# A two-layer hybrid encoder step: pairs of half products written as a software pipeline, with one fixed order each on PE, ACT and DVE

## The chip, the cores and the metric

One core of a Trainium2 chip runs the whole program. The metric is the device time of one execution in microseconds; the median of three timed runs counts, and a separate execution was profiled.

## What is computed

One inference step of an encoder of two layers (D_MODEL = 1024) for 512 prompt rows and 8 x 16 sample rows, 640 rows in all (T), which share the weights. Cut to what matters here, a layer is

```python
(a_u, a_v, a_g, b_x, b_g, c_q, c_kv, c_kr, c_g, m_q, gate_logits) = split_cols(x @ w_in)
oa, v_rows = gmlp_branch(a_u, a_v, ...);  oa = oa * silu(a_g)
ob, conv_new, h_new = rglru_branch(b_x, ...);  ob = ob * silu(b_g)
oc, ckv_new, kr_new = mla_branch(c_q, c_kv, c_kr, ...);  oc = oc * silu(c_g)
om = mem_attend(m_q, mem_k, mem_v)
g = sigmoid(gate_logits).reshape(B, T, 4, D_MODEL)
merged = g[:,:,0] * (oa @ w_br[:512]) + g[:,:,1] * (ob @ w_br[512:1024]) \
       + g[:,:,2] * (oc @ w_br[1024:1536]) + g[:,:,3] * (om @ w_br[1536:])
x_new = layer_norm(ALPHA * x + merged @ w_out)
```

Every product is done in float32r with the operands split into a high and a low part (high x high, high x low, low x high).

## The kernel before, in words

All activations lie transposed, features on the partitions and the 640 rows in the free dimension, as two halves of TH = 320 columns. The program is written for the Tile framework: it puts each engine's instructions into an order by its own scheduler, hands out buffers from pools and sets the semaphores; `order_only` adds an order between two instructions, with no data behind it.

**A pair.** `fm_pair` (line 363) makes two chunks of 128 output columns of `x @ w_in` (tensor w_fm) at once, by a Strassen-like scheme of seven half products in place of eight. Each product is 12 matmuls of 128x128 by 320 columns (4 blocks of the contraction; high x high, high x low, low x high), in the order p1 to p7. The products read sums of the halves of x (`xt`), which are made ahead, and these weights: p1 and p2 the first weight tile r0 split into wh (ACT, line 146) and wl (DVE, line 147), written w0 below; p3 and p4 the sum tile ws (w1); p5 and p6 the changed r1 (w2); p7 the 512 columns of the changed second half of r0 (w3). "w3's low part" is the DVE instruction of line 147 that makes the low part of w3, over 512 columns. PSUM holds the results: p1, p2, p3, p5 and p7 in one tile fp, p4 and p6 in fp_c. Between the products ACT copies p1 and u (third product) into tile tu and p4 into z1; DVE (line 389) joins them into z0 and z1. The function `take` then gets each finished part for the activation function.

**40 pairs.** Each layer has six early pairs (`gelu_pair`, `silu_pair`), between the projections and the attention, and 14 merge pairs (`merge_pairs`, line 1055). A merge pair makes the gate logits of chunks f and f+1 of one branch (bi; 4 and 6 in branch 0, 0 to 6 in the other three), ACT applies tanh, and then `merge_y` multiplies the branch's output (bhl, high and low part, made by `bsplit` at the branch's first pair; oscr holds it in DRAM) by the weights of these two chunks (w_br, 512 KB for both; in the last branch w_brm, 256 KB): 48 matmuls or 24, in PSUM tiles y. DVE joins gate and y (lines 1034 and 1038) into macc. "y's tile" is the raw tile of w_br or w_brm, "y's cast" and "y's low part" its split, and "y" the product.

**Weights and their buffers.** Every weight tile comes by a DMA on SP's queue into a tile of the tag raw, and is then split:

```python
def wtile(tag, n, name, bufs=2):
    return wp.tile([128, n], F32 if tag in ("raw", "ws") else F32R, tag=tag, name=name, bufs=bufs)

def wraw(src, n=1024):
    raw = wtile("raw", n, "raw", 3)
    nc.sync.dma_start(out=raw, in_=src)
```

So raw has three buffers, wh three, wl two and ws one, and a load waits until the last reader of the buffer that it gets is done. SP issues its DMAs in order.

**Who sets the order.** On PE the products of all pairs are chained by `order_only`, through `tail["p"]`, in the order of the program. Everything else (ACT, DVE, SP, the matmuls of y) is put in order by the scheduler alone, by what is ready first in its own estimate.

Of the kernel before, what the change touches and what calls it, by code (L numbers as in the profile page):

```python
# [9 lines left out]
F32 = mybir.dt.float32  # L10
F32R = mybir.dt.float32r
AF = mybir.ActivationFunctionType
ALU = mybir.AluOpType
# [6 lines left out]
T = NP_ + NS  # L20
# [19 lines left out]
def encoder_step(  # L40
# [5 lines left out]
    nc = tc.nc  # L46
# [33 lines left out]
    def acc(name="acc"):  # L80
        return pa.tile([128, 2, 512], F32, tag="acc", name=name)

    def bank_s(name="ps_s"):
        return pb.tile([128, 512], F32, tag="s", name=name, bufs=2)
# [85 lines left out]
    def order_only(ins_, dep):  # L170
        if dep is not None:
            tc.add_manual_dep(
                ins_.ins, dep.ins.name,
                mybir.DependencyInfo(mybir.DependencyClass.NoSync, mybir.DependencyReason.SCHED_ONLY),
                reason="products of a pair stand in this order on the engine",
            )
# [23 lines left out]
    for l in range(L):  # L200
# [159 lines left out]
            xt[11], xt[21] = ((xh[i][:, :, lo_], xl[i][:, :, lo_]) for i in range(2))  # L360
            xt[22] = xh[1][:, :, hi_], xl[1][:, :, hi_]

        def fm_pair(c, take):

            r0, r1 = (wraw(ins["w_fm"][l, c + e]) for e in range(2))
            ws = wtile("ws", 1024, "ws", 1)
            a_, b_ = slice(0, 512), slice(512, 1024)

            def wsum(out, x, y):
                DVE.tensor_tensor(out=out, in0=x, in1=y, op=ALU.add)  # L370

            ab, bc = acc("fp"), bank_s("fp_c")[:, 0:TH]
            ba, bb = (ab[:, j, 0:TH] for j in range(2))

            def product(o, hl, half, x, first, last):
                bh, bl = xt[x]
                h, lo = hl
                steps = [(k, h, b) for k in range(4) for b in (bh, bl)] + [(k, lo, bh) for k in range(4)]
                for n, (k, a, b) in enumerate(steps):
                    k0 = half * 512 + k * 128  # L380
                    mm = PE.matmul(  # L381
                        out=o, lhsT=a[:, k0:k0 + 128], rhs=b[:, k, :],
                        start=(first and n == 0), stop=(n == len(steps) - 1), skip_group_check=True,
                    )
                    order_only(mm, tail.get("p"))
                    tail["p"] = mm

            def psum(out, x, y, op):
                DVE.tensor_tensor(out=out, in0=x, in1=y, op=op)  # L389

            z0, z1, t_ = ftmp([128, T], "z0"), ftmp([128, T], "z1"), tmp([128, T], "tu")
            p1, u = t_[:, lo_], t_[:, hi_]
            w1 = whl(r0)
            product(ba, w1, 0, 11, True, False)
            ACT.copy(out=p1, in_=ba)  # L395
            product(bb, w1, 1, 21, True, True)
            psum(z0[:, lo_], p1, bb, ALU.add)
            take(0, lo_, z0[:, lo_])
            wsum(ws[:, b_], r0[:, a_], r1[:, a_])
            wsum(r1[:, a_], r1[:, a_], r1[:, b_])  # L400
            wsum(ws[:, a_], r0[:, a_], r1[:, a_])
            w1 = whl(ws)
            product(ba, w1, 0, 2, False, False)
            ACT.copy(out=u, in_=ba)
            product(bc, w1, 1, 3, True, False)
            ACT.copy(out=z1[:, hi_], in_=bc)
            w1 = whl(r1)
            wsum(r0[:, b_], r0[:, b_], ws[:, a_])
            product(ba, w1, 0, 1, False, False)
            psum(z1[:, hi_], z1[:, hi_], ba, ALU.subtract)  # L410
            product(bc, w1, 1, 4, False, True)
            psum(z1[:, lo_], bc, u, ALU.subtract)
            take(1, slice(0, T), z1)
            w4 = whl(r0[:, b_], 512)
            product(ba, w4, 0, 22, False, True)
            take(0, hi_, ba)
            return z0, z1

        def silu_pair(i, c, fm):
            gs = []  # L420
            z = fm_pair(fm + c, lambda e, cols, v_: gs.append((e, cols, v_)))
            th = [tmp([128, T], f"th{e}") for e in range(2)]
            for e, cols, v_ in gs:
                ACT.activation(out=th[e][:, cols], in_=v_, func=AF.Tanh, scale=0.5)
                DVE.scalar_tensor_tensor(
                    out=th[e][:, cols], in0=th[e][:, cols], scalar=1.0, in1=v_, op0=ALU.add, op1=ALU.mult
                )
            for e in range(2):
                nc.gpsimd.dma_start(out=gscr[i][c + e], in_=th[e])

        def gelu_pair(c):
            gs = []
            z = fm_pair(FM_U + c, lambda e, cols, v_: gs.append((e, cols, v_)))
            for e, cols, v_ in gs:
                ACT.activation(out=ub[:, c + e, cols], in_=v_, func=AF.Gelu_apprx_tanh)


        a0, a1 = acc("c01"), acc("c23")
# [72 lines left out]

        am = atile([128, 5120], F32, "am")
        ub = am[:, 2560:5120].rearrange("p (k t) -> p k t", k=4)
        for c in (0, 2):
            gelu_pair(c)


        nc.sync.dma_start(out=am[:, 0:1024], in_=ins["w_mix"][l])
# [16 lines left out]
            layer_norm(v[:, t, :], v[:, t, :], mvv[:, t, 0:1], rv[:, t:t + 1], vlg, vlb)  # L535
        nc.gpsimd.dma_start(out=outs["sv"][l], in_=v[:, 4, :])

        silu_pair(1, 0, FM_CG)


        nc.sync.dma_start(out=ckvT_s[:, :, 0:128], in_=ins["past_ckvT"][l])
# [21 lines left out]
                out=krT_s[r:r + 32, :, 128:144], in_=o[r:r + 32, 384:512].rearrange("p (b t) -> p b t", b=NB)  # L563
            )

        silu_pair(1, 2, FM_CG)


        for c in range(4):
# [17 lines left out]
            DVE.tensor_tensor(out=ub[:, c, :], in0=ub[:, c, :], in1=th, op=ALU.mult)  # L587
        nc.gpsimd.dma_start(out=gscr[0].rearrange("k p t -> p k t"), in_=ub)

        for c in (0, 2):  # L590
            silu_pair(2, c, FM_BG)

        ep = otile([128, 2560], F32, "ep")
        nc.sync.dma_start(out=ep[:, 1024:2304], in_=ins["rope_q"])
# [421 lines left out]
        def bsplit(bi, get):  # L1016
            nk, scale = (2, 1.0) if bi == 3 else (4, 0.5)
            if bi == 3:
                t_ = otile([128, 2, nk, T], F32R, "bhl")
                bhl = [t_[:, 0], t_[:, 1]]  # L1020
            else:
                bhl = [otile([128, nk, T], F32R, f"bhl{j}") for j in range(2)]
            for k in range(nk):
                split(bhl[0][:, k, :], bhl[1][:, k, :], get(k), scale)
            return bhl

        def merge_y(bi, f, g, wh, wl, bhl):
# [12 lines left out]
        def merge_split(f):  # L1040
            mg.append(otile([128, 2, 2, T], F32R, f"mg{f}"))
            for e in range(2):
                split(mg[-1][:, 0, e, :], mg[-1][:, 1, e, :], macc[:, f + e, :], 0.5)
# [8 lines left out]
                merge_y(0, f, g, wh, wl, bhl)  # L1052
                yield bhl

        def merge_pairs(bi, fs, bhl=None):
            br, n = (0, 2, 1, 3)[bi], 256 if bi == 3 else 512
            wsrc = ins["w_brm"][l] if bi == 3 else ins["w_br"][l, br]

            def back(k):
                src = tmp([128, T], "osrc")  # L1060
                nc.gpsimd.dma_start(out=src, in_=oscr[br][k])
                return src

            for f in fs:
                gs = []
                z = fm_pair(22 + br * 8 + f, lambda e, cols, v_: gs.append((e, cols, v_)))
                for e, cols, v_ in gs:
                    ACT.activation(out=z[e][:, cols], in_=v_, func=AF.Tanh, scale=0.5)
                if bhl is None:
                    bhl = bsplit(bi, back)  # L1070
                raw = wtile("raw", 2 * n, "raw", 3)
                nc.sync.dma_start(
                    out=raw.rearrange("p (e c) -> p e c", e=2), in_=wsrc[f:f + 2].rearrange("e p c -> p e c")
                )
                wh, wl = whl(raw, 2 * n)
                for e in range(2):
                    c = slice(e * n, (e + 1) * n)
                    merge_y(bi, f + e, z[e], wh[:, c], wl[:, c], bhl)
                if bi == 3 and f == 0:
                    merge_split(0)  # L1080
            if bi == 3:
                for f in (2, 4, 6):
                    merge_split(f)

        lru_in(0)
        lru_split(0)
# [24 lines left out]
        lru_rest(3)  # L1111
        nc.gpsimd.dma_start(out=outs["lh"][l], in_=lh)
        x_sums_back()
        merge_pairs(0, (4, 6), bhl)
        for bi in (1, 2, 3):
            merge_pairs(bi, (0, 2, 4, 6))


        wo = {}
# [187 lines left out]
```

## Time and profile before

| | |
|---|---|
| median of 3 runs | 1473.69 us (1472.77 to 1473.84) |
| profiled execution | 1476.25 us, its span 1474.5 us |
| mean granted TensorE clock | 0.996 |
| PE, PEld | 94%, 85% of the span |
| DVE, ACT, POOL | 67%, 44%, 8% |
| weight loads in the queue of SP | 108 of w_fm, 20 of w_br (512 KB), 8 of w_brm |

The time of an execution is the span of the profile and what lies around it (1.75 us here). PE is the matmuls, PEld the weight loads that run beside them; DVE is VectorE, ACT ScalarE, POOL GpSimd, SP the engine that issues the loads. In the timeline an instruction's row ends with the time that its engine sat idle before it and with what ended that wait; "issue" is a wait for nothing that the profile shows. The layers' merge stages with pairs lie at about 375 to 665 and 1110 to 1410 us of the span.

### The profile page before, as it was taken

How to read it: one execution, taken by the hardware profiler on the slowest of the kernel's cores; microseconds unless marked ns; L12 is line 12 of the kernel's file. 1: busy time of each engine (PE TensorE's matmuls, PEld its weight loads, DVE VectorE, ACT ScalarE, POOL GpSimd, SP SyncE). 2: the span in 40 equal slices, each digit the busy share in tenths (PEclk: the TensorE clock that was granted, in tenths of full speed). 3: DMA queues.
4: the chain of work that ended last, by engine and by line, in shares of the span. 5: the costliest groups of instructions: out<-in, count | busy, mean ns of one | idle time of the engine just before them, and what ended most of it. 6: DMA issues, size and time to landing. Idle time of an engine off the chain costs nothing. (4 is left out here: it accounts for less than half of the span.)

```text
span 1474.5 us, 22634 instructions
## 1 busy us (share of the span) xinstructions
PE 1383.2 (94%) x8896; PEld 1256.6 (85%) x8896; DVE 984.0 (67%) x1676; ACT 650.2 (44%) x1159; POOL 124.5 (8%) x254
## 2 busy tenths in 40 slices
PE   8998899999999999999999989999999999999997
PEld 8788888788989999988888888876889999998886
DVE  8677757685566566665885776575855565657756
ACT  6453534464634343444255435444555433434430
POOL 1101200021100000000111012000211000000000
PEclk9999999999999999999999999999999999999999
DMA  7624523153233322236374247132533323222343
GB/s 273 247 86 168 194 82 118 57 193 123 87 118 104 90 82 80 72 101 207 107 230 184 85 161 230 30 118 83 183 125 97 103 90 104 84 78 60 108 140 107
DMA packets 59098, 183.95 MB, mean 125 GB/s; under 512 B 6641, under 2 KB 15761, under 8 KB 55921
## 3 DMA queue, kind: packets, MB, share of 16 engines
q1 hardware_dynamic: 48304, 127.54, 27.3%
q0 software_dynamic: 10688, 54.98, 10.3%
q8 instruction: 70, 1.15, 0.3%
q14 instruction: 36, 0.29, 0.1%
HBM read 148.49 MB, written 32.69 MB: 123 GB/s over the span
## 5 line engine op out<-in xcount | busy, mean ns | idle before, releaser
L146 ACT CAST wh<-raw 128x1024 fp32r<-128x1024 f32 (+3 forms) x215 | 198.7, 924 | 244.4 <-PE fp_c L381 84.0
L147 DVE TENSOR_TENSOR wl<-raw,wh 128x1024 fp32r<-128x1024 f32 (+3 forms) x215 | 229.1, 1065 | 106.5 <-issue 41.6
L381 PE MATMUL fp<-xh,wh 128*128 128x320 f32 x480 | 147.3, 319 | 27.1 <-ACT tu L395 23.5
L121 PE MATMUL y<-bhl,wh 128*128 128x320 f32 x896 | 142.6, 310 | 4.3 <-ACT lb L905 3.3
L381 PE MATMUL fp<-xl,wh 128*128 128x320 f32 x480 | 142.6, 309 | 0.0
L121 PEld LDWEIGHTS y<-bhl,wh 128*128 128x128 f32 x896 | 134.0, 188 | 5.1 <-ACT lb L905 3.8
L381 PE MATMUL fp<-xt,wh 128*128 128x320 f32 x640 | 110.9, 315 | 26.3 <-DVE z L389 26.3
L381 PEld LDWEIGHTS fp<-xt,wh 128*128 128x128 f32 x640 | 95.5, 188 | 36.7 <-DVE z L389 36.7
L381 PEld LDWEIGHTS fp<-xh,wh 128*128 128x128 f32 x480 | 90.0, 188 | 38.9 <-ACT tu L395 34.0
L121 PE MATMUL fm<-xl,wh 128*128 128x320 f32 x448 | 114.4, 327 | 0.0
L121 PE MATMUL fm<-xh,wh 128*128 128x320 f32 x448 | 111.7, 323 | 0.0
L381 PE MATMUL fp_c<-xt,wh 128*128 128x320 f32 x640 | 106.9, 309 | 0.0
L381 PEld LDWEIGHTS fp_c<-xt,wh 128*128 128x128 f32 x640 | 97.1, 188 | 0.0
L146 ACT CAST wh<-ws 128x1024 fp32r<-128x1024 f32 x40 | 42.1, 1053 | 115.9 <-DVE ws L370 97.2
L381 PEld LDWEIGHTS fp<-xl,wh 128*128 128x128 f32 x480 | 90.2, 188 | 0.1
L381 PE MATMUL fp<-xh,wl 128*128 128x320 f32 x480 | 89.9, 309 | 0.0
L121 PE MATMUL fm<-xh,wl 128*128 128x320 f32 x448 | 87.2, 327 | 0.0
L121 PEld LDWEIGHTS fm<-xh,wh 128*128 128x128 f32 x448 | 75.5, 188 | 6.8 <-issue 5.2
L121 PEld LDWEIGHTS fm<-xl,wh 128*128 128x128 f32 x448 | 76.2, 189 | 5.9 <-issue 4.7
L121 PE MATMUL y<-bhl,wl 128*128 128x320 f32 x448 | 76.6, 309 | 0.0
L381 PEld LDWEIGHTS fp<-xh,wl 128*128 128x128 f32 x480 | 75.3, 188 | 0.0
L121 PEld LDWEIGHTS fm<-xh,wl 128*128 128x128 f32 x448 | 68.8, 190 | 6.3 <-issue 5.9
(339 smaller groups left out, 2632.2 us busy)
## 6 DMA issues: line engine op xcount, KB each, us to landing
raw<-in_w_fm SPq DMA_DIRECT2D x108, 512.0 KB, 3.7
xsum<-xt POOLq DMA_DIRECT2D x8, 1280.0 KB, 11.0
xt<-xsum POOLq DMA_DIRECT2D x8, 1280.0 KB, 7.3
raw<-in_w_br SPq DMA_DIRECT2D x20, 512.0 KB, 3.9
mcache<-in_mem_kv SPq DMA_DIRECT2D x8, 1024.0 KB, 7.0
raw<-in_w_out SPq DMA_DIRECT2D x16, 512.0 KB, 4.5
osrc<-oscr POOLq DMA_DIRECT2D x20, 320.0 KB, 3.3
gscr<-th POOLq DMA_DIRECT2D x16, 320.0 KB, 2.5
```

Of the source, the lines that this page charges most:

```text
L121: PE.matmul(out=out[:, j, 0:TH], lhsT=a(k), rhs=b(k)[:, j * TH:(j + 1) * TH], start=(n == 0), stop=(n == len(steps) - 1),)
L146: ACT.copy(out=dst_h, in_=src)
L147: DVE.tensor_tensor(out=dst_l, in0=src, in1=dst_h.bitcast(F32), op=ALU.subtract)
L381: mm = PE.matmul(out=o, lhsT=a[:, k0:k0 + 128], rhs=b[:, k, :], start=(first and n == 0), stop=(n == len(steps) - 1), skip_group_check=True,)
```

## The change

`fm_pair` is taken apart. A class `Pair` holds a pair's steps: `load` (r0 and r1), `cast0` and `low0` (w0), `sums`, `cast1` and `low1` (w1). `run_pair(p, nxt, act, y)` writes out the products of pair p and, between them, the steps of the next pair nxt up to its cast1. A class `Branch` holds the steps of y: `cast` (the load of its tile and ACT's cast), `low` and `run`. `on(eng, ins)` chains not only PE's instructions but also ACT's and DVE's of the pairs (copies, casts, low parts, sums, differences, activations), each engine in the order of the program. The instructions of y's product, of bhl, of DVE's joins into macc and of the rest of the layer stay with the scheduler. The early pairs are chained the same way, each writing the next one's steps; `silu_pair` and `gelu_pair` hand their activation functions in as `act`. No instruction's shape changes. The core of the diff:

```diff
+        def on(eng, ins_):
+            order_only(ins_, tail.get(eng))
+            tail[eng] = ins_
+            return ins_
...
+        def wcast(src, n):
+            h = wtile("wh", n, "wh", 3)
+            on("ACT", ACT.copy(out=h, in_=src))
+            return h
+
+        def wlow(src, h, n):
+            lo = wtile("wl", n, "wl")
+            on("DVE", DVE.tensor_tensor(out=lo, in0=src, in1=h.bitcast(F32), op=ALU.subtract))
+            return h, lo
...
+        class Pair:
...
+            def load(self):
+                self.r0, self.r1 = (wraw(ins["w_fm"][l, self.c + e]) for e in range(2))
...
+        def first_pair(p):
+            p.load()
+            p.cast0()
+            p.low0()
+            p.sums(0)
+            p.sums(1)
+            p.cast1()
+
+        def run_pair(p, nxt, act, y=None):
...
+            product(ba, p.w0, 0, 11, True, False)
+            copy_out(p1, ba)
+            p.low1()
+            h2 = wcast(r1, 1024)
+            product(bb, p.w0, 1, 21, True, True)
             psum(z0[:, lo_], p1, bb, ALU.add)
...
+            act(0, lo_, z0, z0[:, lo_])
+            w2 = wlow(r1, h2, 1024)
+            wsum(r0[:, b_], r0[:, b_], p.ws[:, a_])
+            product(ba, p.w1, 0, 2, False, False)
+            copy_out(u, ba)
+            h3 = wcast(r0[:, b_], 512)
+            product(bc, p.w1, 1, 3, True, False)
+            copy_out(z1[:, hi_], bc)
+            w3 = wlow(r0[:, b_], h3, 512)
+            if nxt:
+                nxt.load()
+            if y:
+                y.cast()
+            elif nxt:
+                nxt.cast0()
+                nxt.sums(0)
+            product(ba, w2, 0, 1, False, False)
             psum(z1[:, hi_], z1[:, hi_], ba, ALU.subtract)
...
+            if not y and nxt:
+                nxt.sums(1)
+            product(bc, w2, 1, 4, False, True)
             psum(z1[:, lo_], bc, u, ALU.subtract)
...
+            if y:
+                y.low()
+            if nxt:
+                if y:
+                    nxt.cast0()
+                else:
+                    nxt.low0()
+            act(1, slice(0, T), z1, z1)
+            if not y and nxt:
+                nxt.cast1()
+            product(ba, w3, 0, 22, False, True)
+            act(0, hi_, z0, ba)
+            if y:
+                if nxt:
+                    nxt.low0()
+                    nxt.sums(0)
+                    nxt.sums(1)
+                    nxt.cast1()
+                y.run((z0, z1))
...
+        class Branch:
...
+            def cast(self):
+                self.raw = wtile("raw", 2 * self.n, "raw", 3)
+                nc.sync.dma_start(
+                    out=self.raw.rearrange("p (e c) -> p e c", e=2),
+                    in_=self.src[self.f:self.f + 2].rearrange("e p c -> p e c"),
+                )
+                self.h = wcast(self.raw, 2 * self.n)
...
+            first_pair(ps[0])
+            for n, y in enumerate(ys):
...
+                run_pair(ps[n], ps[n + 1] if n + 1 < len(ps) else None, act, y)
```

What the scheduler and the pools make of it shows at two places. In the rows a tile's number tells one tile of a name from another.

The first is SP's queue in the merge stage of the first layer, at the first pair of branch 1 and the ones behind it: SP's loads before.

```order
L1072 DMA raw_5245<-in_w_br 128x2x512
L103 DMA raw_5305<-in_w_fm 128x1024
L103 DMA raw_5307<-in_w_fm 128x1024
L1072 DMA raw_5428<-in_w_br 128x2x512
L103 DMA raw_5488<-in_w_fm 128x1024
L103 DMA raw_5490<-in_w_fm 128x1024
```

The same pairs of loads in the change:

```order
L103 DMA raw_5187<-in_w_fm 128x1024
L103 DMA raw_5189<-in_w_fm 128x1024
L1141 DMA raw_5191<-in_w_br 128x2x512
L103 DMA raw_5388<-in_w_fm 128x1024
L103 DMA raw_5390<-in_w_fm 128x1024
L1141 DMA raw_5392<-in_w_br 128x2x512
```

Before, raw_5428 is y's tile of the pair whose r0 and r1 are raw_5305 and raw_5307, and it is issued directly behind them; now y's tile raw_5392 of the pair of raw_5187 and raw_5189 stands behind the two loads of the pair that follows (raw_5388 and raw_5390).

The second place is ACT, in that first pair of branch 1, from the copy of u (tu) on: before,

```order
L404 COPY tu_5113<-fp_5109 128x320
L149 ACTIVATE bhl0_5227<-osrc_5237 128x640
L146 CAST wh_5247<-raw_5245 128x1024
L406 COPY z1_5112<-fp_c_5110 128x320
L149 ACTIVATE bhl0_5227<-osrc_5241 128x640
L146 CAST wh_5315<-raw_5305 128x1024
L1068 ACTIVATE z1_5112<-z1_5112 128x640
L1068 ACTIVATE z0_5111<-fp_5109 128x320
```

and in the change:

```order
L375 COPY tu_5122<-fp_5118 128x320
L379 CAST wh_5170<-raw_5004 128x512
L149 ACTIVATE bhl0_5247<-osrc_5257 128x640
L149 ACTIVATE bhl0_5247<-osrc_5261 128x640
L375 COPY z1_5121<-fp_c_5119 128x320
L379 CAST wh_5193<-raw_5191 128x1024
L379 CAST wh_5223<-raw_5187 128x1024
L1172 ACTIVATE z1_5121<-z1_5121 128x640
L1172 ACTIVATE z0_5120<-fp_5118 128x320
```

y's cast (wh_5247 before, wh_5193 in the change) moved from ahead of the copy of fp_c to behind it, and the cast of w3's 512 columns, which stood further up before, now lies between the copy of u and the third and fourth bhl.

## Rows read from the trace of the kernel before

**Rows 1.** The page's part 1: busy time, share of the span and instructions of each engine.

```profile
PE 1383.2 (94%) x8896; PEld 1256.6 (85%) x8896; DVE 984.0 (67%) x1676; ACT 650.2 (44%) x1159; POOL 124.5 (8%) x254
```

**Rows 2.** Windows: each engine's busy us (x instructions), PEclk, DMA share, GB/s, both merge stages.

```profile
450.00:670.00 220.00, 205.82 (x1366) 200.03 (x1365) 142.08 (x186) 89.42 (x133) 3.22 (x6) 1.00 0.28 86
1190.00:1410.00 220.00, 205.50 (x1363) 199.69 (x1362) 141.33 (x185) 89.06 (x133) 2.69 (x5) 1.00 0.29 89
```

**Rows 3.** Waits of PE, whole run: us in total, times, longest us.

```profile
PE fp L381 <- DVE z L389: 28.8, 41, 1.5
PE fp L381 <- ACT tu L395: 23.5, 36, 1.3
```

**Rows 4.** Timeline, PEld and PE of one pair: start, us, engine, line, [idle before <-releaser].

```profile
1211.52 0.19 PEld L381 LDWEIGHTS fp<-xh,wh 128*128 128x128 f32 x1
...
1214.10 0.41 PE L381 MATMUL fp<-xh,wh 128*128 128x320 f32 x1 [0.52 <-ACT tu L395]
...
1216.77 1.44 PE L381 MATMUL fp<-xt,wh 128*128 128x320 f32 x8 [0.65 <-DVE z L389]
...
1225.54 2.39 PEld L121 LDWEIGHTS y<-bhl,wh 128*128 128x128 f32 x16
...
1232.58 0.19 PEld L381 LDWEIGHTS fp<-xh,wh 128*128 128x128 f32 x1
```

**Rows 5.** Lines by form, ACT in five periods: busy us, mean ns, idle before.

```profile
L146 ACT CAST wh<-raw 128x1024 fp32r<-128x1024 f32 x16 | 16.8, 1052 | 24.4 <-PE fp_c L381 13.3 <-PE y L121 11.0 <-ACT bhl L149 0.2
...
L146 ACT CAST wh<-raw 128x512 fp32r<-128x512 f32 x5 | 3.1, 620 | 7.8 <-PE fp L381 7.8
```

**Rows 6.** Timeline, SP (start of an issue, its us), the same pair and the next.

```profile
1204.76 0.38 SPq L1072 DMA_DIRECT2D raw<-in_w_br  x1
...
1218.22 0.33 SPq L103 DMA_DIRECT2D raw<-in_w_fm  x1
...
1221.38 0.33 SPq L103 DMA_DIRECT2D raw<-in_w_fm  x1
...
1225.81 0.38 SPq L1072 DMA_DIRECT2D raw<-in_w_br  x1
```

**Rows 7.** Timeline, DVE, the same pair: w2's, w3's and y's low parts.

```profile
1216.64 1.22 DVE L147 TENSOR_TENSOR wl<-raw,wh 128x1024 fp32r<-128x1024 f32 x1
1220.66 0.69 DVE L147 TENSOR_TENSOR wl<-raw,wh 128x512 fp32r<-128x512 f32 x1 [2.80 <-issue]
...
1224.53 1.22 DVE L147 TENSOR_TENSOR wl<-raw,wh 128x1024 fp32r<-128x1024 f32 x1
```

**Rows 8.** DMA issues of the whole run: KB each, median us to landing.

```profile
raw<-in_w_fm SPq DMA_DIRECT2D x108, 512.0 KB, 3.7
...
raw<-in_w_br SPq DMA_DIRECT2D x20, 512.0 KB, 3.9
...
raw<-in_w_brm SPq DMA_DIRECT2D x8, 256.0 KB, 2.7
```

**Rows 9.** Line L1072 (loads of w_br), first layer, then second: us to landing.

```profile
DMA to landing us min/median/max: 3.5/3.9/4.6
...
DMA to landing us min/median/max: 3.6/3.9/4.3
```

**Rows 10.** Timelines of SP, DVE and PE at one early pair, and that load's landing.

```profile
143.20 0.33 SPq L103 DMA_DIRECT2D raw<-in_w_fm  x1
DMA to landing us min/median/max: 5.8/5.8/5.8
149.04 0.69 DVE L370 TENSOR_TENSOR ws<-raw 128x512 f32<-128x512 f32 x1 [2.46 <-DMA raw<-in_w_fm]
150.91 0.42 PE L381 MATMUL fp<-xh,wh 128*128 128x320 f32 x1 [1.54 <-DVE z L389]
```

**Rows 11.** Timeline, DVE, the pair of 1253.6, where a branch begins.

```profile
1262.03 0.82 DVE L150 SCALAR_TENSOR_TENSOR bhl<-osrc,bhl 128x640 fp32r<-128x640 f32 x1 [0.48 <-ACT bhl L149]
1262.78 0.69 DVE L147 TENSOR_TENSOR wl<-raw,wh 128x512 fp32r<-128x512 f32 x1
```

More of the change, by code (lines that the diff above doesn't have):

```diff
@@ L361, in x_whole, with wsum @@
             xt[22] = xh[1][:, :, hi_], xl[1][:, :, hi_]
[L363 to L370, printed above, removed]
+        def on(eng, ins_):
+            order_only(ins_, tail.get(eng))
+            tail[eng] = ins_
+            return ins_
+        def wsum(out, x, y):
+            on("DVE", DVE.tensor_tensor(out=out, in0=x, in1=y, op=ALU.add))
@@ new lines, in psum, with copy_out @@
+        def psum(out, x, y, op):
+            on("DVE", DVE.tensor_tensor(out=out, in0=x, in1=y, op=op))
+        def copy_out(out, in_):
+            on("ACT", ACT.copy(out=out, in_=in_))
+        def wcast(src, n):
[6 more added lines that the diff above has]
+            return h, lo
@@ new lines, in encoder_step, with __init__, cast0, low0 @@
+        a_, b_ = slice(0, 512), slice(512, 1024)
+        class Pair:
+            def __init__(self, c):
+                self.c = c
+            def load(self):
+                self.r0, self.r1 = (wraw(ins["w_fm"][l, self.c + e]) for e in range(2))
+            def cast0(self):
+                self.h0 = wcast(self.r0, 1024)
+            def low0(self):
+                self.w0 = wlow(self.r0, self.h0, 1024)
+            def sums(self, n):
+                r0, r1 = self.r0, self.r1
+                if n == 0:
+                    self.ws = wtile("ws", 1024, "ws", 1)
+                    wsum(self.ws[:, b_], r0[:, a_], r1[:, a_])
+                    wsum(r1[:, a_], r1[:, a_], r1[:, b_])
+                else:
+                    wsum(self.ws[:, a_], r0[:, a_], r1[:, a_])
+            def cast1(self):
+                self.h1 = wcast(self.ws, 1024)
+            def low1(self):
+                self.w1 = wlow(self.ws, self.h1, 1024)
@@ new lines, in product @@
+        def product(o, hl, half, x, first, last):
+            bh, bl = xt[x]
+            h, lo = hl
+            steps = [(k, h, b) for k in range(4) for b in (bh, bl)] + [(k, lo, bh) for k in range(4)]
+            for n, (k, a, b) in enumerate(steps):
+                k0 = half * 512 + k * 128
+                on("PE", PE.matmul(
+                    out=o, lhsT=a[:, k0:k0 + 128], rhs=b[:, k, :],
+                    start=(first and n == 0), stop=(n == len(steps) - 1), skip_group_check=True,
+                ))
@@ L372, in fm_pair @@
+        def first_pair(p):
[6 more added lines that the diff above has]
+        def run_pair(p, nxt, act, y=None):
+            r0, r1 = p.r0, p.r1
             ab, bc = acc("fp"), bank_s("fp_c")[:, 0:TH]
             ba, bb = (ab[:, j, 0:TH] for j in range(2))
[L375 to L386, printed above, removed]
@@ L388, in psum @@
-            def psum(out, x, y, op):
-                DVE.tensor_tensor(out=out, in0=x, in1=y, op=op)
             z0, z1, t_ = ftmp([128, T], "z0"), ftmp([128, T], "z1"), tmp([128, T], "tu")
             p1, u = t_[:, lo_], t_[:, hi_]
[L393 to L396, printed above, removed]
-            psum(z0[:, lo_], p1, bb, ALU.add)
-            take(0, lo_, z0[:, lo_])
-            wsum(ws[:, b_], r0[:, a_], r1[:, a_])
@@ L400, in fm_pair @@
[L400 to L409, printed above, removed]
+            product(ba, p.w0, 0, 11, True, False)
+            copy_out(p1, ba)
@@ L410, in fm_pair @@
+            if nxt:
[6 more added lines that the diff above has]
+            product(ba, w2, 0, 1, False, False)
             psum(z1[:, hi_], z1[:, hi_], ba, ALU.subtract)
-            product(bc, w1, 1, 4, False, True)
+            if not y and nxt:
+                nxt.sums(1)
+            product(bc, w2, 1, 4, False, True)
             psum(z1[:, lo_], bc, u, ALU.subtract)
-            take(1, slice(0, T), z1)
@@ L414, in fm_pair @@
[L414 to L421, printed above, removed]
-            th = [tmp([128, T], f"th{e}") for e in range(2)]
-            for e, cols, v_ in gs:
-                ACT.activation(out=th[e][:, cols], in_=v_, func=AF.Tanh, scale=0.5)
-                DVE.scalar_tensor_tensor(
+            if y:
+                y.low()
@@ new lines, in run_pair @@
+            if nxt:
+                if y:
+                    nxt.cast0()
+                else:
+                    nxt.low0()
[11 more added lines that the diff above has]
+                y.run((z0, z1))
@@ new lines, in gelu_pair, with act, silu_pair @@
+        def gelu_pair(p, nxt):
+            def act(e, cols, z, v_):
+                on("ACT", ACT.activation(out=ub[:, p.c - FM_U + e, cols], in_=v_, func=AF.Gelu_apprx_tanh))
+            run_pair(p, nxt, act)
+        def silu_pair(p, nxt, i, c):
+            th = [tmp([128, T], f"th{e}") for e in range(2)]
+            rest = []
+            def act(e, cols, z, v_):
+                on("ACT", ACT.activation(out=th[e][:, cols], in_=v_, func=AF.Tanh, scale=0.5))
+                rest.append((e, cols, v_))
+            run_pair(p, nxt, act)
+            for e, cols, v_ in sorted(rest, key=lambda r: -r[0]):
+                on("DVE", DVE.scalar_tensor_tensor(
@@ L426, in silu_pair @@
                     out=th[e][:, cols], in0=th[e][:, cols], scalar=1.0, in1=v_, op0=ALU.add, op1=ALU.mult
-                )
+                ))
             for e in range(2):
                 nc.gpsimd.dma_start(out=gscr[i][c + e], in_=th[e])
[L431 to L435, printed above, removed]
@@ L513, in encoder_step @@
         ub = am[:, 2560:5120].rearrange("p (k t) -> p k t", k=4)
-        for c in (0, 2):
-            gelu_pair(c)
+        ps = [Pair(f + c) for f in (FM_U, FM_CG, FM_BG) for c in (0, 2)]
+        first_pair(ps[0])
+        for n in range(2):
+            gelu_pair(ps[n], ps[n + 1])
         nc.sync.dma_start(out=am[:, 0:1024], in_=ins["w_mix"][l])
@@ L536, in encoder_step @@
         nc.gpsimd.dma_start(out=outs["sv"][l], in_=v[:, 4, :])
-        silu_pair(1, 0, FM_CG)
+        silu_pair(ps[2], ps[3], 1, 0)
         nc.sync.dma_start(out=ckvT_s[:, :, 0:128], in_=ins["past_ckvT"][l])
@@ L564, in encoder_step @@
             )
-        silu_pair(1, 2, FM_CG)
+        silu_pair(ps[3], ps[4], 1, 2)
         for c in range(4):
@@ L588, in encoder_step @@
         nc.gpsimd.dma_start(out=gscr[0].rearrange("k p t -> p k t"), in_=ub)
-        for c in (0, 2):
-            silu_pair(2, c, FM_BG)
+        silu_pair(ps[4], ps[5], 2, 0)
+        silu_pair(ps[5], None, 2, 2)
         ep = otile([128, 2560], F32, "ep")
@@ L1053, in merge_whole, with __init__, low, back @@
                 yield bhl
[L1055 to L1059, printed above, removed]
+        class Branch:
+            def __init__(self, bi, f, bhl=None):
+                self.bi, self.f, self.n = bi, f, 256 if bi == 3 else 512
+                self.br = (0, 2, 1, 3)[bi]
+                self.src = ins["w_brm"][l] if bi == 3 else ins["w_br"][l, self.br]
+            def cast(self):
[5 more added lines that the diff above has]
+                self.h = wcast(self.raw, 2 * self.n)
+            def low(self):
+                self.hl = wlow(self.raw, self.h, 2 * self.n)
+            def back(self, k):
@@ L1060, in back, with run @@
                 src = tmp([128, T], "osrc")
-                nc.gpsimd.dma_start(out=src, in_=oscr[br][k])
+                nc.gpsimd.dma_start(out=src, in_=oscr[self.br][k])
                 return src
[L1064 to L1075, printed above, removed]
-                for e in range(2):
-                    c = slice(e * n, (e + 1) * n)
-                    merge_y(bi, f + e, z[e], wh[:, c], wl[:, c], bhl)
-                if bi == 3 and f == 0:
+            def run(self, z):
+                wh, wl = self.hl
+                if self.bi not in bhls:
+                    bhls[self.bi] = bsplit(self.bi, self.back)
+                for e in range(2):
+                    c = slice(e * self.n, (e + 1) * self.n)
+                    merge_y(self.bi, self.f + e, z[e], wh[:, c], wl[:, c], bhls[self.bi])
@@ new lines, in encoder_step, with merge_pairs, act @@
+        bhls = {}
+        def merge_pairs(bhl):
+            bhls[0] = bhl
+            ys = [Branch(0, f) for f in (4, 6)] + [Branch(bi, f) for bi in (1, 2, 3) for f in (0, 2, 4, 6)]
+            ps = [Pair(22 + y.br * 8 + y.f) for y in ys]
+            first_pair(ps[0])
+            for n, y in enumerate(ys):
+                def act(e, cols, z, v_):
+                    on("ACT", ACT.activation(out=z[:, cols], in_=v_, func=AF.Tanh, scale=0.5))
+                run_pair(ps[n], ps[n + 1] if n + 1 < len(ps) else None, act, y)
+                if y.bi == 3 and y.f == 0:
@@ L1080, in merge_pairs @@
                     merge_split(0)
-            if bi == 3:
-                for f in (2, 4, 6):
-                    merge_split(f)
+            for f in (2, 4, 6):
+                merge_split(f)
         lru_in(0)
@@ L1113, in encoder_step @@
         x_sums_back()
-        merge_pairs(0, (4, 6), bhl)
-        for bi in (1, 2, 3):
-            merge_pairs(bi, (0, 2, 4, 6))
+        merge_pairs(bhl)
         wo = {}
```

## The prediction

> **What bounds the kernel now.** I read the busy shares first: PE is busy 94% of the span and DVE 67% [rows 1], so what can change the time is PE's order or a wait of PE. The windows show the same for the two stages that hold most of the 28 merge pairs: PE works 205.8 and 205.5 of 220 us there, at a granted clock of 1.00, which is the upper of the two levels (2.4 GHz), so there is no clock to win or lose [rows 2]. PE's waits in the whole run name two places: 28.8 us for DVE's z and 23.5 us for ACT's tu [rows 3]. The timeline of one merge pair shows that both are built into the pair: the second product waits 0.52 us for ACT's copy of p1, the third 0.65 us for z out of the bank that p1 and p2 share [rows 4]. 40 pairs by 1.17 us are 46.8 of the 52.3 us; only 5.5 us are waits that a better order could remove.
>
> That pair is my clock for the rest. It starts at 1211.52, its y at 1225.54, and the next pair at 1232.58: 21.06 us [rows 4]. So y is needed 14.0 us after the pair's start, with no gap on PE before it.
>
> **What the edit does to PE itself: nothing.** It adds and removes no matmul, copy, cast or sum. p1's copy still stands between the first two products, and z between the second and third; both waits remain, 0 us won or lost. The casts and low parts also stay the same in number, at 1.05 us for 1024 columns and 0.62 for 512 on ACT [rows 5]; DVE has a third of the span free, which covers them. If that cover were gone it would show as a wait of PE for wl.
>
> **What it does to the loads of y's weights.** The buffers of raw decide this. There are three, and each merge pair loads three tiles: its two w_fm tiles r0 and r1 and y's tile of w_br. Before, SP issues y's tile, then the next pair's r0 and r1. The rows show how early: y's tile for the pair of 1211.52 goes out at 1204.76, and the next one's at 1225.81, 7 us ahead of the next pair's start and 21 us before its y; the two w_fm loads go out in the middle of the pair, at 1218.22 and 1221.38 [rows 6]. Each is released by the last reader of a buffer: the first follows w2's low part (1216.64 + 1.22 = 1217.86), the second w3's low part, which ends at 1220.66 + 0.69 = 1221.35 [rows 7]. So now the last buffer to come free goes to the next pair's r1, which is read only by the sums that stand behind y's low part, from 1224.53 + 1.22 = 1225.75 on.
>
> After, SP's order is r0 and r1 of the next pair, then y's tile of the *current* pair. Of the three buffers the previous y's goes to r0, the one behind w2's low part to r1, and the only one left for y's tile is that of the current r0, whose last reader is w3's low part. Thus y's load is issued where r1's was, at 1221.38. The w_fm loads become earlier (no gain, they had time); y's becomes 16.6 us later against its use.
>
> **Its price per pair.** w3's low part cannot run sooner: it waits for the buffer that the fourth product reads, and stands right behind that product's end in both orders. From 1221.38 a w_br tile lands in 3.9 us (median of 20 [rows 8]; the ends of the two layers are 3.5 and 4.6 [rows 9]). A consumer started 0.04 us after a landing: issue 143.20, landing 5.8 us later, DVE's sum at 149.04 [rows 10]. ACT's cast of 1024 columns takes 1.05 us [rows 5]; PE's first y matmul reads it. 1221.38 + 3.9 + 0.04 + 1.05 = 1226.37, against the 1225.54 at which PE is ready for y: **0.83 us of stall**. By the shortest landing (3.5) it is 0.43, by the longest (4.6) 1.53. I take 3.9, since the loads that are issued at this point now (r1, 512 KB too) have a median of 3.7 among all w_fm loads [rows 8], so this place in the pair is not a bad one, and w_br's own median is nearer than either end.
>
> The stall does not grow from pair to pair: PE starts the next pair later by as much, and with it everything that the load waits for. Nor is it hidden: PE's order is fixed and y stands next.
>
> The 28 merge pairs split by their weights. In 20 of them w_br has 512 KB: 20 x 0.83 = 16.6 us. In the other 8 w_brm has 256 KB, landing after 2.7 us [rows 8], and the cast has 512 columns: 1221.38 + 2.7 + 0.04 + 0.62 = 1224.74, 0.8 us before it is needed: 0.
>
> In four of the 20 a new branch begins, and its split into bhl runs within the same pair. On DVE three of its four operations stand ahead of w3's low part, in both orders; the third waits 0.48 us for ACT and ends just as w3's low part begins, at 1262.78 [rows 11], 9.15 us into its pair, 42.1 us behind the pair above and no later in it. On ACT, however, the cast of 512 columns now stands between the copy of u and the third bhl, where the copy stood directly ahead of it. The third comes 0.62 us later [rows 5], and with it w3's low part and y's load: 4 x 0.6 = 2.4 us more (ends 0 and 2.5).
>
> **What queues behind that wait.** ACT now waits in front of y's cast until about 1225.3. Behind it stand the next pair's cast of r0 and the two tanh; the tanh have 640 and 320 columns, so each takes less than the 1.05 us of the cast of 1024 (an estimate from that row), and all three end before 1226.37 + 3 x 1.05 = 1229.5. The bank that the last tanh reads is wanted by the second half of y, 3.5 us after y's start (half of 1225.54 to 1232.58), that is at 1229.9. On DVE, y's low part starts behind y's cast and ends at 1226.37 + 1.22 = 1227.6; PE wants it after 16 loads, 2.39 us [rows 4], at 1228.8. So only the cast reaches PE. On SP nothing is held back: the loads behind y's tile wait for y's own low part.
>
> **The early pairs (6 in each layer)** have no y. Their loads keep their places: r1 of the next pair behind w2's low part, and the two sums ahead of the difference for z1, as before. 0, with one risk, below.
>
> **What is won.** At most the 5.5 us of waits beyond the built-in ones. One row of them is a late load and not an order: an early pair's r1 took 5.8 us, and PE stood 1.54 us at the seventh product [rows 10]. I take a quarter, 1.4 us, and keep 0 and 5.5 as ends.
>
> **The sum:** 16.6 + 2.4 - 1.4 = 17.6 us. The profiled execution took 1476.25 us (span 1474.5 and 1.75 around it), 2.56 over the median of the runs, 1473.69; the terms come out of that one execution but carry over unchanged: 1473.69 + 17.6 = **1491** us.
>
> The Trainium skill ("DMA: Bandwidth & Descriptors", section on rules for kernel authors) asks for a DMA to be issued early and waited for late. It speaks against this change where y's tile is concerned and for it where the w_fm tiles are. The same page ("Anatomy of one DMA", SWDGE path) fits a transfer as 2.0 us and the bytes at 436 GB/s, which for 512 KB is an estimate of 3.2 us; the sum by that fit would be 20 x 0.13 + 2.4 - 1.4, some 3.6 us. The fit is for another queue than SP's, and no w_br load here was that short: the shortest is 3.5.
>
> **The rivals.**
> *A. The load is fast enough and nothing changes.* PE feels nothing if the tile lands within 1225.54 - 1.05 - 0.04 - 1221.38 = 3.07 us. For: the queue would hold little else then, since the w_fm loads are already done. Against: y's loads of before had the queue nearly to themselves too (the previous issue lies 4.4 us back, 1221.38 to 1225.81 [rows 6]) and still took 3.5 to 4.6. Time 1473.7, within 1471 to 1477 (the page's fit would belong at its upper edge or just above). Chance 0.06.
> *B. Faster.* y's tile comes in time, or its wait eats into a wait elsewhere, and the fixed order on ACT and DVE removes what exceeds the built-in waits. For: 5.5 us are there [rows 3]. Against: it needs the load within 3.07 us in nearly all 20 pairs; the point that decides is a landing of 3.07 us at no more than 3 or 4 misses. Time 1473.7 - 5.5 = 1468. Chance 0.05.
> *C. Slower than I think.* In the ten early pairs that have a successor the sums for it stand on DVE ahead of the difference that frees PE's bank; the one late landing of before cost 1.54 us [rows 10]. If the fixed order makes this the rule it is 10 x 1.54 = 15 us on top: 1506. Against: the order at this place is the same as before, where 1 pair in 12 paid. Chance 0.09.
>
> **How the numbers follow.** My case has a chance of 0.80, with 1481 to 1501 of its own (20 landings that average 3.6 to 4.3 us give 0.53 to 1.23 us each, so 10.6 to 24.6, with bhl's 2.4 and the gain's 0 to 5.5). The range reaches from 1478, the shortest landing in every pair (8.6 us) with most of the gain, to 1506, the longest one in nearly every pair or most of C. Some 3 us, 0.2%, are what a measurement can tell from no change. Faster 0.05 (B), same 0.06 (A), slower 0.89.
>
> **What would show it.** In the profile after: PE (and PEld) of y waits for ACT's wh some 20 times, about 0.8 us each, in all 15 to 20 us, where now y waits for nothing there; ACT's cast of raw names the DMA of w_br as its releaser; SP issues w_br right after w3's low part, about 9.9 us into the pair; the merge period is about 21.9 us with w_br and unchanged in the last four pairs of a layer; the waits of fp for z and tu stay near 47 us. I am wrong if y's line shows no wait for wh, if w_br still goes out a pair ahead, or if the time went into the early pairs or the attention part, where I expect less than 2 us.

## The result, and the profile after

The change made the kernel slower: 1489.12 us, the median of four runs (1487.40 to 1489.98), against 1473.23 us for the kernel before in the same job; the ratio is 1.0111, with a 95% interval of 1.0093 to 1.0130. That is 15.9 us. The profiled execution took 1489.98 us, its span 1488.2, 13.7 us over the span before.

The page's part 1 of the kernel after (busy time, share of the span, instructions) answers to [rows 1]; the two windows (busy us of PE, PEld, DVE, ACT and POOL, then PEclk, DMA share, GB/s) answer to [rows 2]:

```profile
PE 1390.5 (93%) x8896; PEld 1257.4 (84%) x8896; DVE 985.9 (66%) x1676; ACT 637.8 (43%) x1159; POOL 124.3 (8%) x254
```

```profile
450.00:670.00 220.00, 202.47 (x1330) 194.67 (x1328) 137.41 (x180) 82.02 (x127) 3.22 (x6) 1.00 0.27 85
...
1190.00:1410.00 220.00, 202.38 (x1330) 194.76 (x1329) 137.39 (x179) 81.61 (x127) 3.23 (x6) 1.00 0.28 85
```

The matmuls are the same 8896 and the clock in these windows is 1.00 as before; PE gets through 1330 of them in a window where it did 1366 and 1363. So PE waits more. The waits of PE's weight loads, in the whole run (us in total, times, longest), say for what:

```profile
PEld fp L423 <- DVE z L372: 40.8, 45, 1.7
PEld fp L423 <- ACT tu L375: 32.5, 38, 1.6
PEld y L121 <- ACT wh L379: 17.9, 20, 2.6
```

The third row is new: 20 waits of y for its cast weights, as many as there are w_br pairs. Before, y waited for other things, and these two rows are gone:

```profile
PEld y L121 <- ACT lb L905: 3.8, 2, 1.9
PEld y L121 <- ACT z L1068: 1.2, 1, 1.2
```

For PE's matmuls the two old rows stand nearly as in [rows 3]:

```profile
PE fp L423 <- DVE z L372: 29.1, 42, 1.5
PE fp L423 <- ACT tu L375: 22.4, 36, 1.3
PE y L121 <- ACT wh L379: 12.7, 20, 2.3
```

(PE's own row for y is shorter than PEld's: at the wait in the pair below PE counts 0.19 us idle and PEld 0.45, since the last matmuls end later than their weight loads; the pair becomes longer by PEld's figure.) One ordinary pair, from several views of the timeline, answers to [rows 4 to 7]:

```profile
1199.82 0.19 PEld L423 LDWEIGHTS fp<-xh,wh 128*128 128x128 f32 x1
...
1208.96 0.69 DVE L384 TENSOR_TENSOR wl<-raw,wh 128x512 fp32r<-128x512 f32 x1 [2.21 <-PE fp_c L423]
1209.68 0.38 SPq L1141 DMA_DIRECT2D raw<-in_w_br  x1
...
1213.22 2.00 ACT L379 CAST wh<-raw 128x1024 fp32r<-128x1024 f32 x2 [3.91 <-DMA raw<-in_w_br]
...
1214.32 2.34 PEld L121 LDWEIGHTS y<-bhl,wh 128*128 128x128 f32 x16 [0.45 <-ACT wh L379]
1214.32 2.61 PE L121 MATMUL y<-bhl,wh 128*128 128x320 f32 x16 [0.19 <-ACT wh L379]
...
1221.31 0.19 PEld L423 LDWEIGHTS fp<-xh,wh 128*128 128x128 f32 x1
```

The pair starts at 1199.82. w3's low part begins 9.14 us later and ends at 1209.65; SP issues y's tile at 1209.68; ACT, which had waited 3.91 us for that DMA, starts the two casts (y's and the next r0's) at 1213.22, 3.54 us after the issue; the first is done 1.05 us later, and y starts 0.45 us after PE's last weight load was done. The period is 21.49 us, where it was 21.06 [rows 4].

The twenty waits are of three kinds. Fourteen lie between 0.45 and 0.67 us (7.6 us in all); the four at a branch's start between 1.42 and 1.48 (5.8 us); the first merge pair of each layer, 2.08 and 2.55 (4.6 us). One of the last two kinds each:

```profile
1147.20 3.23 PEld L121 LDWEIGHTS y<-bhl,wh 128*128 128x128 f32 x16 [2.55 <-ACT wh L379]
...
1192.82 2.35 PEld L121 LDWEIGHTS y<-bhl,wh 128*128 128x128 f32 x16 [1.43 <-ACT wh L379]
```

From the first merge pair to the output projection the profile measures 285.3 and 283.9 us in the two layers before, and 292.9 and 294.6 after: 18.4 us more. The rest of the span is 4.7 us shorter. So the whole loss lies in the merge stages. The 17.9 us of waits are nearly all of it. The last four pairs became 1.2 us shorter over both layers, with the wait of 1.2 us for z gone. In the profiled execution the clock also fell to the lower of its two levels for part of 6 us behind the wait of 2.55 us (PEclk, the third number from the end, is a mean over 3 us):

```profile
1147.00:1150.00 3.00, 2.80 (x14) 2.80 (x15) 2.82 (x3) 2.06 (x4) 1.07 (x2) 0.74 0.51 152
1150.00:1153.00 3.00, 3.00 (x17) 3.00 (x16) 1.20 (x3) 0.00 (x0) 0.00 (x0) 0.69 0.66 243
```

y took 8.54 us there, to 1155.74, where the same product of the first layer took 7.00: 1.5 us more. Whether the wait brought the clock down is not shown. 17.9 - 1.2 + 1.5 = 18.2 us.

### The profile page after: what moved, and what is told of

It is laid out like the page before. It is cut to its first block, busy times and chain, and to the rows that moved or that the text cites. A ratio compares the mean times of both kernels' runs of the same rounds, so it can differ in the third digit from the quotient of the medians.

```text
span 1488.2 us, 22595 instructions
## 1 busy us (share of the span) xinstructions
PE 1390.5 (93%) x8896; PEld 1257.4 (84%) x8896; DVE 985.9 (66%) x1676; ACT 637.8 (43%) x1159; POOL 124.3 (8%) x254
## 5 line engine op out<-in xcount | busy, mean ns | idle before, releaser
L384 DVE TENSOR_TENSOR wl<-raw,wh 128x1024 fp32r<-128x1024 f32 (+1 forms) x148 | 153.5, 1049 | 113.6 <-PE fp_c L423 56.7
L379 ACT CAST wh<-raw 128x1024 fp32r<-128x1024 f32 (+1 forms) x148 | 132.3, 910 | 108.8 <-DMA raw<-in_w_br 83.5
L423 PE MATMUL fp<-xh,wh 128*128 128x320 f32 x480 | 147.5, 319 | 24.9 <-ACT tu L375 22.4
L121 PE MATMUL y<-bhl,wh 128*128 128x320 f32 x896 | 145.9, 313 | 12.7 <-ACT wh L379 12.7
L121 PEld LDWEIGHTS y<-bhl,wh 128*128 128x128 f32 x896 | 134.1, 189 | 18.3 <-ACT wh L379 17.9
L375 ACT COPY tu<-fp 128x320 f32<-128x320 f32 x80 | 34.0, 426 | 139.5 <-PE fp L423 138.5
L147 DVE TENSOR_TENSOR wl<-raw,wh 128x1024 fp32r<-128x1024 f32 (+3 forms) x67 | 73.9, 1104 | 20.7 <-ACT wh L146 8.3
L146 ACT CAST wh<-raw 128x1024 fp32r<-128x1024 f32 (+3 forms) x67 | 63.9, 953 | 54.8 <-PE fm L121 17.7
```

Source lines behind the costliest of these rows:

```text
L121: PE.matmul(out=out[:, j, 0:TH], lhsT=a(k), rhs=b(k)[:, j * TH:(j + 1) * TH], start=(n == 0), stop=(n == len(steps) - 1),)
L146: ACT.copy(out=dst_h, in_=src)
L147: DVE.tensor_tensor(out=dst_l, in0=src, in1=dst_h.bitcast(F32), op=ALU.subtract)
L375: on("ACT", ACT.copy(out=out, in_=in_))
L379: on("ACT", ACT.copy(out=h, in_=src))
L384: on("DVE", DVE.tensor_tensor(out=lo, in0=src, in1=h.bitcast(F32), op=ALU.subtract))
```

## The experiments

Two theories stood against each other. Mine: y's tile gets the last of three raw buffers to come free, its load is issued too late, and landing plus cast set the wait. The rival: the fixed order on ACT puts y's cast too late, wherever its load is. Seven kernels were run; each is compared with the kernel before on the same chip (1471.04 us for the first four, 1470.45 for the last three). The ranges that start from 1473 or 1489 us come from the measurement above, where the kernel before took 2.2 us more than in the first four; the ratios do not depend on that.

**y's load first.** In `run_pair`, with `Branch.cast` cut into a load and a cast:

```diff
+            if y:
+                y.load()
             if nxt:
                 nxt.load()
             if y:
                 y.cast()
```

> The changed kernel with one step moved: y's tile is asked for ahead of the next pair's r0 and r1, not behind them; y's cast keeps its place on ACT. My theory (y's load sits behind w3's low part, because it gets the last of three raw buffers): y's tile now gets the buffer of the previous y, SP issues it a pair ahead, and the 20 waits of PE for y's wh (17.9 us on PEld) go; 1489.1 - 17.9 = 1471 us, between 1468 and 1474. The rival (y's cast stands too late in ACT's fixed order, wherever its load is): the waits stay, 1487 to 1491 us.

Measured: 1469.05 us, ratio to before 0.9987 (0.9977 to 0.9997). In the list of PEld's waits y no longer waits for wh at all; the one row left that names an engine is the wait of the first layer's last pair for the gate:

```profile
PEld y L121 <- ACT z L1176: 0.4, 1, 0.4
```

SP issues y's tile 7 us ahead of the pair again, and next to the POOL engine's load of osrc, as it did before:

```profile
1219.14 0.38 SPq L1143 DMA_DIRECT2D raw<-in_w_br  x1
```

The merge stages take 285.3 and 283.8 us, as before the change. y's cast has the same place on ACT as in the changed kernel, so the rival has fallen: the order on ACT costs nothing by itself. By the two ratios the move is worth 1.0111 / 0.9987 = 1.2%, 18 us, about the 17.9 us of waits.

**The kernel before, y's load late.** The loads of the next pair are written into `fm_pair` behind w4's split, ahead of y's; nothing else is fixed:

```diff
             w4 = whl(r0[:, b_], 512)
+            mid()
             product(ba, w4, 0, 22, False, True)
...
+                def mid():
+                    if todo:
+                        pre.append(fm_load(todo.pop(0)))
```

> The kernel before with the loads of the next pair's r0 and r1 written ahead of the load of y's tile, ACT and DVE left to the scheduler. My theory: the load's place alone costs the time, so PE waits some 20 times for y's wh, 0.5 to 0.9 us each, 10 to 18 us in all: 1484 to 1491 us. The rival (the fixed order of ACT and DVE costs it): the load is late but the kernel stays within 3 us of 1473.

Measured: 1482.06 us, ratio 1.0078 (1.0063 to 1.0094), 11.0 us more than before, which is 2 us under the range that I gave as a time and within the 10 to 18 us. PEld's row:

```profile
PEld y L121 <- ACT wh L146: 14.1, 20, 1.9
```

The late load alone, with ACT and DVE left to the scheduler, makes the twenty waits, though not their full 17.9 us.

**PE's chain only.** `on` chains PE's instructions and no others:

```diff
-            order_only(ins_, tail.get(eng))
-            tail[eng] = ins_
+            if eng == "PE":
+                order_only(ins_, tail.get(eng))
+                tail[eng] = ins_
```

> The changed kernel without the chains on ACT and DVE; PE's chain and the written order of the loads stay. My theory: the late load stays and with it the waits for y's wh, 10 to 18 us over the kernel before: 1484 to 1492 us. The rival (the fixed order on ACT and DVE costs it): 1470 to 1476 us, as before.

Measured: 1480.73 us, ratio 1.0070 (1.0056 to 1.0083). As a time this is in neither range, 3 us below mine and 5 above the rival's; over the kernel before on the same chip it is 9.7 us, just under my 10 to 18. The waits are there, in the list and, at a branch's start, in the timeline:

```profile
PEld y L121 <- ACT wh L380: 14.1, 19, 1.7
```

```profile
1187.68 2.34 PEld L121 LDWEIGHTS y<-bhl,wh 128*128 128x128 f32 x16 [0.92 <-ACT wh L380]
```

So the late load costs some 10 us and the fixed order on ACT and DVE some 6 more on top of it (0.0041 of the ratio is 6; the merge stages are 7.7 us shorter here than in the changed kernel, of which 1.5 are that kernel's stretch of lower clock). The profile says where: a branch's start waits 0.80 to 0.97 us where it was 1.42 to 1.48, because the scheduler does not put the cast of 512 columns ahead of the third bhl; the first pairs wait 1.67 and 1.74 instead of 2.08 and 2.55; and the last four pairs are shorter, by 2.9 us over both layers. Why these last are shorter was not pursued.

**y's tile in halves.** The load and the cast stay in their places, as two of 256 KB and 512 columns:

```diff
+                for e in range(2):
+                    c = slice(e * self.n, (e + 1) * self.n)
+                    nc.sync.dma_start(out=self.raw[:, c], in_=self.src[self.f + e])
+                for e in range(2):
+                    c = slice(e * self.n, (e + 1) * self.n)
+                    on("ACT", ACT.copy(out=self.h[:, c], in_=self.raw[:, c]))
```

> The changed kernel with y's tile loaded and cast in two halves of 256 KB and 512 columns, in the same places. My theory (landing plus cast of the first operand set the wait): a first half lands in about 2.7 us and its cast takes 0.62, together 1.3 to 1.4 us sooner than now, so the 14 waits of about 0.5 us go, the four of 1.44 at a branch's start shrink to about 0.1 and the two of the first pairs to about 1: some 15 us less, 1473 to 1478 us. The rival (place in ACT's order): at most the shorter cast helps, 20 x 0.43 = 9 us, 1480 us or more.

Measured: 1469.50 us, ratio 0.9993 (0.9984 to 1.0002), 3.5 us under my range as a time. SP still issues y's tile behind w3's low part, and ACT still waits for it, but only 2.98 us where it was 3.91; each half takes 0.62 us:

```profile
1214.90 0.80 SPq L1144 DMA_DIRECT2D raw<-in_w_br  x2
...
1217.51 1.26 ACT L1147 CAST wh<-raw 128x512 fp32r<-128x512 f32 x2 [2.98 <-DMA raw<-in_w_br]
```

In the whole run y waits once for wh:

```profile
PEld y L121 <- ACT wh L1147: 0.7, 1, 0.7
```

The time from issue to the end of the first cast is what decided: 3.54 + 1.05 = 4.59 us before the halving, 1217.51 + 0.62 - 1214.90 = 3.2 us with it, against the 4.2 us that PE leaves (1214.32 - 0.45 - 1209.68). My range was too high because I kept a rest of 0.1 us at the branch starts and of 1 us at the first pairs; of these the 0.7 us are left, and two waits for y's low part of 1.1 us in all.

**The two waits called built in.** So far p1 and p2 stand in the two halves of one PSUM tile, fp (2 x 512 columns). Here the second product goes to a tile of its own, first in the kernel of the first experiment, then in the kernel before:

```diff
-            ba, bb = (ab[:, j, 0:TH] for j in range(2))
+            ba, bb = ab[:, 0, 0:TH], bank_t("fp_b")[:, 0:TH]
```

> The kernel of e1_y_load_first (y's load first) with the second half product written into a PSUM bank of its own, not into the other half of fp. It tests the two waits that I called built in. If they come from the shared tile fp, as I hold, p2 no longer waits for ACT's copy of p1 nor p3 for DVE's z: 40 x 1.17 us of PE idle at least, 40 x 1.69 us by PEld at most, so 1469 - 47 to - 67 = 1402 to 1422 us. The rival (p3 and p5 then run into the next wait, for DVE's low parts or ACT's copies): half of it or less, 1436 us or more.

Measured: 1419.66 us, ratio 0.9650 (0.9633 to 0.9667): inside the range.

> The kernel before with the second half product in a PSUM bank of its own, nothing else changed. If the two waits are built in by the shared tile alone, they go here too: 1471 - 47 to - 67 = 1404 to 1424 us, within 5 us of e5_y_first_own_bank. If the fixed order of ACT and DVE is needed to use the room, this one stays over 10 us behind it.

Measured: 1412.04 us, ratio 0.9609 (0.9595 to 0.9624), the fastest kernel here, 58 us under the kernel before by one line. It is inside the range too, and 7.6 us ahead of the other one, where I had them within 5: the fixed order of ACT and DVE is not needed for it, and is behind. In the profiles the merge stages of both take the same (258.5 and 258.1 us there, 258.1 and 257.6 here), so the difference lies outside of them; why was not pursued. In its profile the wait for ACT's copy is gone from the list of PE's waits, and that for z is down from 28.8 us [rows 3] to

```profile
PE fp L381 <- DVE z L389: 3.9, 4, 1.9
```

and the merge pair is down to 1183.50 - 1164.14 = 19.36 us, with no wait of PE in it; that is 132 matmuls of 0.147 us:

```profile
1164.14 0.19 PEld L381 LDWEIGHTS fp<-xh,wh 128*128 128x128 f32 x1
...
1176.46 2.39 PEld L121 LDWEIGHTS y<-bhl,wh 128*128 128x128 f32 x16
...
1183.50 0.19 PEld L381 LDWEIGHTS fp<-xh,wh 128*128 128x128 f32 x1
```

**y's load first, PE's chain only.** The first experiment with the edit of the third:

> e1_y_load_first without the chains on ACT and DVE, the written order of the loads kept. My theory: with y's load early the fixed order on ACT and DVE has nothing left to cost or give beyond what lies outside the pairs: 1466 to 1474 us, no wait of PE for y's wh. The rival (the chains themselves win the 2 us that e1_y_load_first has over the kernel before): 1471 us or more.

Measured: 1469.69 us, ratio 0.9997 (0.9988 to 1.0005). With y's load early the chains on ACT and DVE are worth 0.6 us by the times, 1.5 by the ratios, or nothing: the intervals of this kernel and of the first overlap. Where the loads are early, the fixed order neither costs nor gives anything that these runs can tell.

## Why the prediction was right, point by point

**The load's place, right.** SP issues y's tile 0.03 us after w3's low part ends, 9.86 us into the pair, as worked out from 1221.38 - 1211.52. The first experiment and the second, the one removing and the other adding this step alone, show it as the cause: the first takes back the whole loss, the second makes 11 us of it, and the fixed order lengthens the waits that a late load makes. Whether a fourth raw buffer would do the same as the earlier place was not run.

**The landing, mis-sized.** I took 3.9 us, the median before, and held that this place in the pair was no better and no worse. From the same place the ordinary pairs' loads landed in 3.5 to 3.7 us. I held, too, that y's loads of before had the queue nearly to themselves, and looked at SP's queue alone. The trace of before has the difference in it: 14 of its 20 w_br loads were issued 0.7 to 1.0 us behind a load of osrc on POOL's queue, and these took 3.8 to 4.6 us; of the other six, five took 3.5 or 3.6 and one 4.0. Moved back, the ordinary pairs' load no longer meets osrc. POOL's load before, ahead of SP's at 1204.76 [rows 6], and after, behind the landing of SP's of 1209.68:

```profile
1204.08 0.54 POOL L1061 DMA_DIRECT2D osrc<-oscr  x1 [20.51 <-ACT wh L146]
...
1213.42 0.54 POOL L1152 DMA_DIRECT2D osrc<-oscr  x1 [21.93 <-issue]
```

In the first experiment, where they meet again (14 loads, 0.63 us behind osrc), these loads took 3.6 to 4.0 us. After, the four at a branch's start landed in 3.9 us and the two first ones, beside POOL's spills (oscr) and a load of osrc, in 4.4. Here are an ordinary, a branch-starting and a first pair's load of the kernel after:

```profile
DMA to landing us min/median/max: 3.5/3.5/3.5
...
DMA to landing us min/median/max: 3.9/3.9/3.9
...
DMA to landing us min/median/max: 4.4/4.4/4.4
```

That osrc's load is the reason was read from the traces, not tried by itself. The wait per ordinary pair came out at 0.54 us on average where I had 0.83, so 20 of them are 10.8 us, not 16.6.

**The branch's start, mis-sized.** I had 0.6 us more in each of the four; it was 1.44 - 0.54 = 0.9. About 0.5 of it is the cast of 512 columns ahead of the third bhl: it goes when ACT is left to the scheduler (1.44 against some 0.9). The other 0.4 is the landing of 3.9 instead of 3.5. In all 3.6 us, not 2.4.

**The first pairs, not foreseen.** The waits of 2.08 and 2.55 us are 3.5 us more than two ordinary ones. Two things delay their y. The loads fall into the spills of the stage before and land some 0.9 us later. And w3's low part, behind which the load is issued, stands on DVE behind work of that stage (lines 1034 to 1039): it begins 1.26 us after the copy of the fourth product does, where in the ordinary pair it is 0.07 (1208.96 against 1208.89).

```profile
1139.72 0.43 ACT L375 COPY z<-fp_c 128x320 f32<-128x320 f32 x1 [0.87 <-PE fp_c L423]
...
1140.98 0.69 DVE L384 TENSOR_TENSOR wl<-raw,wh 128x512 fp32r<-128x512 f32 x1
```

So the sentence that w3's low part stands right behind the fourth product's end held for the ordinary pairs and not for these two.

**The gain elsewhere, too small and looked for in the wrong place.** I took 1.4 us, out of the 5.5 by which fp's waits exceeded the built-in ones. Those waits fell by 0.8 us only (52.3 to 51.5); the late load of the early pair cost 0.91 us where it was 1.54. What went were y's waits for lb ahead of the merge stages, 3.8 us; they are gone in the first and fourth experiments too, but still there where PE alone is chained and in both kernels with a tile of its own for p2; why was not pursued. In all the profile shows 4.7 us outside the merge stages. Only part of it belongs to the change: the profiled execution of before lies 2.6 us over its median, and the kernel of the first experiment, whose merge stages are as long as before, is 2.0 us faster than before (0.4 to 3.4). So I hold to some 2 us.

10.8 + 3.6 + 3.5 = 17.9 us of waits, less 2, are the 15.9 us measured; the forecast had 17.6. That it came so near is partly luck: the ordinary pairs' term was 5.8 us too large, and the two terms for the branches' starts and the first pairs together 4.7 too small.

**The part with no effect, right.** The w_brm pairs did not wait; the two waits of fp for z and tu stayed (29.1 and 22.4 us of PE); in the early pairs PE's waits in front of fp add up to 12.7 us where they were 14.0. The rivals fell: the load did not land in 3.07 us, so nothing hid it, and the early pairs did not become slower. The Trainium skill ("DMA: Bandwidth & Descriptors", section "Anatomy of one DMA") would have given 3.2 us for 512 KB, an estimate from its fit for another queue; for y's tiles of w_br the trace disagrees, since the shortest of their landings was 3.5, while the two loads of w_uqn, 512 KB on SP's queue too, have a median of 3.2 in the same profile.

**The built-in waits, wrong in a point that the sum did not need.** I wrote that p1 and p2 share a bank and that the two waits are built into the pair. They share the tile fp, each product in its own half, and with a tile of its own for p2 nearly all of these waits went. They are in both kernels alike, so the forecast of the difference did not suffer.

## What to carry to other kernels

When a software pipeline writes the next step's loads ahead of the current step's, ask which buffer each load gets: with three buffers and three loads in a step, the last one asked for waits for the last reader, and that one should be the load that is used last. A wait of 0.5 us per pair came from one line's place, and went by moving the load up or by halving the first piece that PE needs. And before fixing an order, look at the waits that every pair has: a PSUM tile shared by two products cost 58 us here, while the order on ACT and DVE gave 0.6 to 1.5 us or nothing.

## What the runs showed of the hardware that was not expected

The same load of 512 KB landed in 3.5 to 3.7 us in the ordinary pairs after, and in 3.8 to 4.6 us before and 3.6 to 4.0 in the first experiment, where POOL's queue had issued 320 KB up to 1 us ahead of it: a median taken in one place of the program is not the median of the next. A PSUM tile of 2 x 512 columns that two products share cost 1.70 us a merge pair by the period (21.06 against 19.36), where PE's rows showed 0.52 + 0.65 = 1.17 us idle and those of its weight loads 0.78 + 0.91 = 1.69: the waits of PE were only the lower bound.
